# Chunk spacing, accumulator banks and the order of small vector work in a hybrid S5 and retention layer

## The chip, the core and the metric

The kernel runs on one NeuronCore of a Trainium2 chip. The metric is the device time of one execution in microseconds (us); the kernel before has a median of 1449.79 us over three runs (1449.29 to 1450.3). The engines are called by the names of the profile: PE (matmul), DVE (vector), ACT (scalar), POOL (GpSimd) and SP (here used for issuing DMAs).

## The reference

One layer of a decoder is computed for 256 prompt positions and for 8 sequences of 8 decode positions, 320 token columns in all, in float32. The shape of the work, cut to what matters here:

```python
h = rms_norm(x, norm_mix)
u, q, k, v, g = split(h @ w_in)                      # 2048 x 5120
bu = einsum('nlgh,gph->lngp', ug, ((lam_bar-1)/lam)[..., None] * b)
xs = associative_scan(a = lam_bar, bu)               # complex diagonal state, 64 groups x 64
y = gelu(Re(c @ xs) + d*u);  s5_out = y * sigmoid(y @ w_glu + b_glu)
o = chunked retention with decay (8 heads, rotary q and k), group norm, silu(g) gate
x = x + concat([s5_out, ret_out]) @ w_out            # 2048 x 2048
x = x + (silu(h2 @ w_gate) * (h2 @ w_up)) @ w_ffn_out  # 2048 x 2*5632, then 5632 x 2048
y = rms_norm(x);  the last S5 and retention states are returned too
```

Weights are fetched as float32 and split into two parts (`hi`, `lo`); each product is the sum of three matmuls (hi by hi, hi by lo, lo by hi).

## The kernel before

**Dense products.** `gemm` (L137) goes through 128-row tiles of the contraction, called k-steps here. A k-step is three matmuls of 128x128 by 320 columns (L143 to L145). `wload` (L122) issues a 512 KB load of 8 k-steps of weights on SP, a cast to `hi` on ACT (L131) and the subtraction that gives `lo` on DVE (L133). There are three buffers each of raw, `hi` and `lo`, so weights run at most three tiles ahead of PE. An output tile accumulates in a PSUM bank of the pool `ps_acc`, tag "acc", with two buffers.

**The stages in order.** First the input projection: a head (L917 to L943) that computes four output tiles together (two S5 inputs, q and k of head 0) as x and the weights arrive; then v of head 0, and the loop L985 over eight heads with q, k, v, for the first four heads also the gate g, for the first six also one S5 input tile u; then the last four gates. Second the first half of the output projection, `ps_o`, on the retention rows: `gemm_late` (L151) takes its first two output tiles together and goes through heads 0 to 3 of both before heads 4 to 7 of both. Third the GLU product, the second half of the output projection, and the FFN.

**What is woven between.** During the input projection, PE also does the small matmuls of the retention heads (`head_k` L711, `head_v` L736) and of eight S5 chunks (`s5_chunk` L575). PE's and POOL's orders are written out by hand: a planner keeps a clock, `clk.now`, that each matmul advances by a fixed cost (0.4 for a k-step); a generator that yields a number of units is resumed at the first k-step boundary after its due time (`run_due`, L91). Chunk c is due to start at `T0 + PER*c` (L978). From its start it yields `b1` = 14.2 (then `pt`, transposes of the input matrix `bl`), `b2` = 6.6 (then `pb`, the product with the inputs `kst`, and `pk_`, the local kernel `toe`), `scan` = 17.8 (then `py`, the output product) and `y` = 10 (then the elementwise end). When the input projection is over, a loop (L1010) runs the planner on, without dense work between, until chunk 7 is done; only then the output projection is written to PE's stream. The DVE, ACT and SP orders are not fixed by hand: the framework orders them when the program is built, by program order less an offset where one is given (`tc.high_priority`), and by `tc.issue_after`, which puts a block behind a named instruction on its engine. An engine executes its queue in that order.

**PSUM.** Eight banks: two for `ps_acc`; three for `ps_m`, tag "misc", which hold the small results of heads and chunks (`pst`, `pss`, `pst2`, `psr`, `pn`, `pt`, `pk_`, the norm sums, and the v product of head 0); one for `ps_v` (`po`); two for `ps_b` (`pb` and `py` in turn). In the head, `py0` is a "misc" bank, `pb0` the two of `ps_b`, and `pk0` an "acc" bank beside that of the warming matmuls.

**S5 parameters and tables.** `s5_params` (L382), `s5_params2` (L422) and `s5_params3` (L444) make the powers of the transition from small tiles, on DVE; `s5_params2` stands behind the scaling of the rotary tables (L969), `s5_params3` behind the scores of head 0 (L732). `first_states` (L468) is six POOL multiplications and additions that the planner starts at `T0 + 1`. `s5_table` (L517) makes a chunk's rotation table with six DVE operations, right behind its matrices (L612).

**The first loads.** ACT issues the parameter vector `vec` (L918) and the second k-step's weights, SP the first k-step's x, the first weights, and all further loads.

Of the kernel before, what the change touches and what calls it, by code (L numbers as in the profile page):

```python
# [12 lines left out]
F32 = mybir.dt.float32  # L13
# [5 lines left out]
PSUM = bass.MemoryType.PSUM  # L19

P = 128
# [3 lines left out]
N = NP + NB * NS  # L25
# [19 lines left out]
def hybrid_kernel(ctx, tc, xT, w_in, w_in4, w_out, w_glu, w_fi, w_fo, vecs, s5p, bc, x0,  # L45
# [3 lines left out]
    pe, act, dve, pool, sp = nc.tensor, nc.scalar, nc.vector, nc.gpsimd, nc.sync  # L49

    cst = ctx.enter_context(tc.tile_pool(name="cst", bufs=1))
    wp = ctx.enter_context(tc.tile_pool(name="wp", bufs=1))
    ps_acc = ctx.enter_context(tc.tile_pool(name="ps_acc", bufs=2, space=PSUM))

    def f(t):
        return t.bitcast(F32)
# [8 lines left out]
    vec = cst.tile([P, vecs.shape[1]], F32, name="vec")  # L65
# [18 lines left out]
    clk = Clk()  # L84
# [6 lines left out]
    def run_due(flush=False):  # L91
        while clk.heap and (flush or clk.heap[0][0] <= clk.now):
            t, _, gen = heapq.heappop(clk.heap)
            clk.now = max(clk.now, t)
            try:
                d = next(gen)
            except StopIteration:
                continue
            spawn(gen, d)
# [11 lines left out]

    def keep_warm(n):

        pt = ps_acc.tile([P, 512], F32, name="warm_ps", tag="acc", bufs=2)
        for _ in range(n):
            pe.matmul(pt, onesr, onesr.unsqueeze(1).to_broadcast([P, 4, P]), start=True, stop=True)

# [19 lines left out]
    def gemm(name, src, nk, xhi, xlo, ps=None, ws=None):  # L137
        ws = ws or wload(src, nk)
        if ps is None:
            pt = ps_acc.tile([P, 512], F32, name=name, tag="acc", bufs=2)  # L140
            ps = pt[:, :N]
        for k, (hi, lo) in enumerate(ws):
            pe.matmul(ps, hi, xhi[:, k], start=k == 0, stop=False)  # L143
            pe.matmul(ps, hi, xlo[:, k], start=False, stop=False)  # L144
            pe.matmul(ps, lo, xhi[:, k], start=False, stop=k == nk - 1)  # L145
            clk.now += 0.4
            if k < nk - 1:
                run_due()
        return ps

    def gemm_late(name, src, n0, ks, nk, xhi, xlo):  # L151

        ws = [wload(src(n0 + i), nk) for i in range(2)]
        pss = []
        for k0, k1 in ((0, ks), (ks, nk)):
            for i in range(2):
                if not k0:
                    pss.append(ps_acc.tile([P, 512], F32, name=name, tag="acc", bufs=2)[:, :N])
                for k in range(k0, k1):
                    hi, lo = ws[i][k]  # L160
                    pe.matmul(pss[i], hi, xhi[:, k], start=k == 0, stop=False)
                    pe.matmul(pss[i], hi, xlo[:, k], start=False, stop=False)
                    pe.matmul(pss[i], lo, xhi[:, k], start=False, stop=k == nk - 1)
                    clk.now += 0.4
                    if k < nk - 1:
                        run_due()
        return pss


    def ts(out, a, s1, o1, s2=None, o2=None):  # L170
        if o2 is None:
            dve.tensor_scalar(out, a, s1, None, o1)
        else:
            dve.tensor_scalar(out, a, s1, s2, o1, o2)
        return out

    def tt(out, a, b, op):
        dve.tensor_tensor(out, a, b, op)  # L178
        return out
# [51 lines left out]
    retpool = ctx.enter_context(ExitStack())  # L231
# [1 line left out]
    xgstack = ExitStack()  # L233
    xg = xgstack.enter_context(tc.tile_pool(name="xg", bufs=1))
    mp = retpool.enter_context(tc.tile_pool(name="mp", bufs=1, side="right"))
    ps_m = retpool.enter_context(tc.tile_pool(name="ps_m", bufs=3, space=PSUM))
    ps_v = retpool.enter_context(tc.tile_pool(name="ps_v", bufs=1, space=PSUM))
    up = retpool.enter_context(tc.tile_pool(name="up", bufs=1, side="right"))
    s5 = s5stack.enter_context(tc.tile_pool(name="s5", bufs=1, side="right"))
# [1 line left out]
    ps_b = s5stack.enter_context(tc.tile_pool(name="ps_b", bufs=1, space=PSUM))  # L241

    def misc(name):
        return ps_m.tile([P, 512], F32, name=name, tag="misc", bufs=3)

    xhi = xg.tile([P, KT, N], F32R, name="xhi")
    xlo = xg.tile([P, KT, N], F32R, name="xlo")
# [86 lines left out]
    def T(shape):  # L334
        n = int(np.prod(shape[1:]))
        a = scr[0][:, scr[1]:scr[1] + n]
        scr[1] += n
        if len(shape) == 3:
            a = a.rearrange("p (a b) -> p a b", b=shape[2])
        return a  # L340
# [81 lines left out]
    def s5_params2(used):  # L422
        newscr(1)
        scr[1] = used
        tt(lp[:, 0, 0], rr, ec[:, 0], MUL)
        tt(lp[:, 1, 0], rr, es[:, 0], MUL)
        den = tt(T(sh), prm[:, 0], prm[:, 0], MUL)
        d2 = tt(T(sh), prm[:, 1], prm[:, 1], MUL)
        tt(den, den, d2, ADD)
        rden = T(sh)  # L430
        dve.reciprocal(rden, den)
        nr = ts(T(sh), lp[:, 0, 0], -1.0, ADD)
        t1 = tt(T(sh), nr, prm[:, 0], MUL)
        t2 = tt(T(sh), lp[:, 1, 0], prm[:, 1], MUL)
        tt(t1, t1, t2, ADD)
        tt(ff[:, 0], t1, rden, MUL)
        t3 = tt(T(sh), lp[:, 1, 0], prm[:, 0], MUL)
        t4 = tt(T(sh), nr, prm[:, 1], MUL)
        tt(t3, t3, t4, SUB)
        tt(ff[:, 1], t3, rden, MUL)  # L440
        r2 = tt(T(sh), rr, rr, MUL)
        tt(r4, r2, r2, MUL)

    def s5_params3():  # L444
        def cmul(o, a, b, shape, tt=tt):

            u1, u2 = T(shape), T(shape)
            tt(u1, a[0], b[0], MUL)
            tt(u2, a[1], b[1], MUL)
            tt(o[0], u1, u2, SUB)  # L450
            tt(u1, a[0], b[1], MUL)
            tt(u2, a[1], b[0], MUL)
            tt(o[1], u1, u2, ADD)

        def ri(t, i):
            return (t[:, 0, i], t[:, 1, i])

        def rep_(t, n):
            return tuple(t[:, q].unsqueeze(1).to_broadcast([P, n, NPAIR]) for q in range(2))

        cmul(ri(lp, 1), ri(lp, 0), ri(lp, 0), sh)
        cmul(ri(lp, slice(2, 4)), rep_(lp[:, :, 1], 2), ri(lp, slice(0, 2)), [P, 2, NPAIR])
        cmul(ri(gp, slice(0, 3)), rep_(ff, 3), ri(lp, slice(0, 3)), [P, 3, NPAIR])

        def b8(a):
            return a.unsqueeze(2).to_broadcast(shx)

        def first_states():  # L468

            yield max(0.0, T0 + 1.0 - clk.now)  # L470
            newscr(0)
            cmul((lx0[:, 0], lx0[:, 1]), (x0t[:, 0], x0t[:, 1]), (b8(lp[:, 0, 3]), b8(lp[:, 1, 3])), shx,
                 pool.tensor_tensor)

        spawn(first_states())
# [99 lines left out]
    def s5_chunk(c):  # L575
# [14 lines left out]
        raw = raws[c]  # L590
# [7 lines left out]
        for w_, pc in ((0, gpc), (1, lpc)):  # L598
# [10 lines left out]
                continue  # L609
            tt(cl[:, 0], m1[:, 0:4], m2[:, 4:8], SUB)  # L610
            tt(cl[:, 1], m1[:, 4:8], m2[:, 0:4], SUB)
        tbl = s5_table(c)  # L612
        yield DL["b1"] + (4.0 if c == 0 else 0.0)
        bst = s5.tile([P, 4, P], F32, name="bst", tag="bst", bufs=1)
        pt = misc("pt")
        for i in range(4):
# [77 lines left out]
    rot_t = {}  # L694
# [197 lines left out]
    def do_g(h):  # L892
        ps = proj(11 + 4 * h)
        sg = mp.tile([P, N], F32, name="sg", tag="sg", bufs=2)
        with tc.high_priority(offset=EVAC):
# [5 lines left out]

    DL = dict(b1=14.2, b2=6.6, scan=17.8, y=10.0, k=8.5, v=6.1,
              o=2.2, u=6.0, c=10.0, n2=2.4, n2b=2.6, nm=0.8)
    T0, PER = 53.6, 33.4


    clk.now = 8.0
# [1 line left out]
    warm = cst.tile([P, 1], F32, name="warm")  # L909
    act.activation(warm, ones[:, 0:1], AF.Silu)  # L910

    py0 = misc("py0")
    pb0 = ps_b.tile([P, 2, 512], F32, name="pb0", tag="pb", bufs=1)
    keep_warm(8)
    pk0 = ps_acc.tile([P, 512], F32, name="ps_p", tag="acc", bufs=2)
    accs = [py0[:, :N], pb0[:, 0, :N], pb0[:, 1, :N], pk0[:, :N]]
    with tc.high_priority(offset=100000), tc.manual_schedule(engines={mybir.EngineType.SP}):  # L917
        act.dma_start(vec, vecs)  # L918
    k0, los = 0, []
    for k1 in (1, *range(2, KT + 1, 2)):  # L920
        with tc.high_priority(offset=100000), tc.manual_schedule(engines={mybir.EngineType.SP}):
            if k0 % 2 == 0:
                raw, hi, lo = (wp.tile([P, 8, P], d, name=n, tag=n, bufs=3).rearrange("p (k o) m -> p k o m", o=4)
                               for n, d in (("raw", F32), ("hi", F32R), ("lo", F32R)))
            q = slice(k0 % 2, (k1 - 1) % 2 + 1)
            sp.dma_start(xrs[k0 // 4][:, k0 % 4:(k1 - 1) % 4 + 1], xT[:, k0:k1])
            (act if k0 == 1 else sp).dma_start(raw[:, q], w_in4[:, k0:k1])
            if k1 == 4:
                sp.dma_start(prm, s5p)
            split_x(k0, k1)  # L930
            act.copy(hi[:, q], raw[:, q])
            los.append(dve.tensor_tensor(lo[:, q], raw[:, q], f(hi[:, q]), SUB))
        if k1 == 4:
            exps = s5_exps()
        if k1 % 2 == 0:
            with tc.high_priority(offset=50000):
                accq = square_x(k1 - 2, k1)
        for k in range(k0, k1):
            for w_, x_ in ((hi, xhi), (hi, xlo), (lo, xhi)):
                for i, ps in enumerate(accs):  # L940
                    pe.matmul(ps, w_[:, k % 2, i], x_[:, k], start=k == 0 and w_ is hi and x_ is xhi,
                              stop=k == KT - 1 and w_ is lo)
            clk.now += 1.6  # L943
        k0 = k1
# [384 lines left out]
```

## Time and profile before

| what | value |
|---|---|
| median of three runs | 1449.79 us |
| the profiled execution | 1448.5 us |
| its span, first to last instruction | 1446.7 us |
| PE busy | 1427.1 us (99%) |
| DVE busy | 849.1 us (59%) |
| ACT busy | 600.7 us (42%) |
| mean granted TensorE clock | 0.995 |

The span is what the trace shows; the execution's own time has 1.8 us around it. Busy time of PE counts overlapping, modelled matmul spans, so that idle time is read from the waits and from the starts of successive matmuls. A timeline row gives the start, the length of the stretch of that group, the engine, the line, the output and inputs, the shape and, in brackets, how long the engine sat idle before and what ended it.

### The profile page before, as it was taken

What the parts mean: (1) busy time and instruction counts of PE and PEld (TensorE: products, weight loads), DVE (VectorE), ACT (ScalarE), POOL (GpSimd) and SP (SyncE); (2) the same over time, 40 slices, a digit from 0 to 9 for tenths busy, and PEclk for the clock granted to TensorE, in tenths of its full rate; (3) what the DMA queues carried; (4) which work ended last, traced back from release to release, by engine and by line L of the source; (5) the groups of instructions that cost most, each with busy time, mean ns of one, the idle gap of its engine ahead of it and who ended that gap; (6) DMA issues with size and microseconds to landing.
All of it is one profiled execution on the core that took longest, in us unless ns stands there. A gap on an engine that the chain in (4) does not pass through costs nothing.

```text
span 1446.7 us, 25879 instructions
## 1 busy us (share of the span) xinstructions
PE 1427.1 (99%) x10434; PEld 1413.5 (98%) x10434; DVE 849.1 (59%) x1378; ACT 600.7 (42%) x945; POOL 75.1 (5%) x161
## 2 busy tenths in 40 slices
PE   9999999998999999999999999999999999999997
PEld 9999999998999999999999999999999999999996
DVE  8978877786566746565444444444444444444454
ACT  7645555554355533333333333333333333333452
POOL 7610000010000000000000000000000000000001
PEclk9999999999999999999999999999999999999998
DMA  8555555555544576664445445444445444444542
GB/s 290 167 162 167 156 172 157 170 155 178 160 154 151 186 222 189 219 202 162 146 152 155 121 145 182 150 146 152 125 149 169 157 154 146 140 138 143 156 145 111
DMA packets 92774, 235.09 MB, mean 163 GB/s; under 512 B 26480, under 2 KB 40432, under 8 KB 92656
## 3 DMA queue, kind: packets, MB, share of 16 engines
q1 hardware_dynamic: 91600, 231.06, 50.3%
q10 hardware_dynamic: 1056, 2.40, 0.5%
q8 instruction: 82, 1.34, 0.4%
q14 instruction: 36, 0.29, 0.1%
HBM read 220.66 MB, written 10.26 MB: 160 GB/s over the span
## 4 chain that ended last, share of the span: by engine, by line
PE 70%; DVE 0%; issue 0%; ACT 0%; DVEq 0%
PE ps_fg L143 7%; PE ps_fo L145 7%; PE ps_fu L145 7%; PE ps_fg L145 7%; PE ps_fo L144 7%; PE ps_fu L144 7%; PE ps_fu L143 7%; PE ps_fg L144 7%; PE ps_fo L143 7%; PE ps_o L144 1%; PE ps_o L143 1%; PE ps_o L145 1%; PE ps_g L144 1%; PE ps_g L145 1%; PE ps_g L143 1%; DVE x L178 0%
## 5 line engine op out<-in xcount | busy, mean ns | idle before, releaser
L133 DVE TENSOR_TENSOR lo<-raw,hi 128x1024 fp32r<-128x1024 f32 (+1 forms) x416 | 467.0, 1123 | 384.0 <-ACT hi L131 383.0
L131 ACT CAST hi<-raw 128x1024 fp32r<-128x1024 f32 (+1 forms) x416 | 401.8, 967 | 683.1 <-PE ps_fo L144 189.3
L143 PE MATMUL ps_fg<-hhi,hi 128*128 128x320 f32 x704 | 217.6, 309 | 0.0
L144 PE MATMUL ps_fo<-alo,hi 128*128 128x320 f32 x704 | 217.5, 309 | 0.0
L145 PE MATMUL ps_fo<-ahi,lo 128*128 128x320 f32 x704 | 217.5, 309 | 0.0
L143 PE MATMUL ps_fo<-ahi,hi 128*128 128x320 f32 x704 | 217.5, 309 | 0.0
L145 PE MATMUL ps_fg<-hhi,lo 128*128 128x320 f32 x704 | 217.4, 309 | 0.0
L144 PE MATMUL ps_fu<-hlo,hi 128*128 128x320 f32 x704 | 217.4, 309 | 0.0
L143 PE MATMUL ps_fu<-hhi,hi 128*128 128x320 f32 x704 | 217.4, 309 | 0.0
L145 PE MATMUL ps_fu<-hhi,lo 128*128 128x320 f32 x704 | 217.4, 309 | 0.0
L144 PE MATMUL ps_fg<-hlo,hi 128*128 128x320 f32 x704 | 217.4, 309 | 0.0
L143 PE MATMUL ps_p<-xhi,hi 128*128 128x320 f32 x560 | 177.8, 318 | 1.3 <-DVE q__1070 L178 1.3
L145 PE MATMUL ps_p<-xhi,lo 128*128 128x320 f32 x560 | 173.1, 309 | 0.0
L144 PE MATMUL ps_p<-xlo,hi 128*128 128x320 f32 x560 | 172.9, 309 | 0.0
L144 PEld LDWEIGHTS ps_fg<-hlo,hi 128*128 128x128 f32 x704 | 132.4, 188 | 0.4
L143 PEld LDWEIGHTS ps_fg<-hhi,hi 128*128 128x128 f32 x704 | 132.3, 188 | 0.3
L143 PEld LDWEIGHTS ps_fu<-hhi,hi 128*128 128x128 f32 x704 | 132.4, 188 | 0.0
L144 PEld LDWEIGHTS ps_fu<-hlo,hi 128*128 128x128 f32 x704 | 132.4, 188 | 0.0
L145 PEld LDWEIGHTS ps_fu<-hhi,lo 128*128 128x128 f32 x704 | 132.4, 188 | 0.0
L145 PEld LDWEIGHTS ps_fg<-hhi,lo 128*128 128x128 f32 x704 | 132.3, 188 | 0.0
L143 PEld LDWEIGHTS ps_fo<-ahi,hi 128*128 128x128 f32 x704 | 132.2, 188 | 0.0
L144 PEld LDWEIGHTS ps_fo<-alo,hi 128*128 128x128 f32 x704 | 132.2, 188 | 0.0
(420 smaller groups left out, 1909.9 us busy)
## 6 DMA issues: line engine op xcount, KB each, us to landing
raw<-w_fi SPq DMA_DIRECT2D x176, 512.0 KB, 3.7
raw<-w_in SPq DMA_DIRECT2D x79, 512.0 KB, 3.9
raw<-w_fo SPq DMA_DIRECT2D x64, 512.0 KB, 3.5
raw<-w_out SPq DMA_DIRECT2D x32, 512.0 KB, 3.7
raw<-w_fo SPq DMA_DIRECT2D x64, 192.0 KB, 2.4
rt<-r SPq DMA_DIRECT2D x8, 512.0 KB, 4.9
raw<-w_glu SPq DMA_DIRECT2D x8, 512.0 KB, 3.5
raw<-r SPq DMA_DIRECT2D x8, 512.0 KB, 4.3
```

Source lines behind the costliest of these rows:

```text
L131: cast = act.copy(hi[:, :m], raw[:, :m])
L133: dve.tensor_tensor(lo[:, :m], raw[:, :m], f(hi[:, :m]), SUB)
L143: pe.matmul(ps, hi, xhi[:, k], start=k == 0, stop=False)
L144: pe.matmul(ps, hi, xlo[:, k], start=False, stop=False)
L145: pe.matmul(ps, lo, xhi[:, k], start=False, stop=k == nk - 1)
```

## The change

- `PER`, the spacing of the S5 chunks on the planner's clock, goes from 33.4 to 32.0.
- `ps_acc` has three buffers, `ps_m` two. `py0` of the head moves from "misc" to "acc".
- The second half of `s5_params2` (eleven small DVE operations that make `ff` and `r4`) moves to the beginning of `s5_params3`, which stands behind the scores of head 0.
- For chunk 0, `s5_table` is called after the chunk's first yield.
- `first_states` is due at `T0 + 12` on the planner's clock in place of `T0 + 1`.
- ACT issues the first k-step's weights; `vec` and the second k-step's weights go to SP, `vec` behind the first x.

```diff
-    ps_acc = ctx.enter_context(tc.tile_pool(name="ps_acc", bufs=2, space=PSUM))
+    ps_acc = ctx.enter_context(tc.tile_pool(name="ps_acc", bufs=3, space=PSUM))
...
-    ps_m = retpool.enter_context(tc.tile_pool(name="ps_m", bufs=3, space=PSUM))
+    ps_m = retpool.enter_context(tc.tile_pool(name="ps_m", bufs=2, space=PSUM))
...
         dve.reciprocal(rden, den)
+        rot_t["rden"] = rden
+
+    def s5_params3():
+        rden = rot_t["rden"]
         nr = ts(T(sh), lp[:, 0, 0], -1.0, ADD)
...
         tt(r4, r2, r2, MUL)
 
-    def s5_params3():
         def cmul(o, a, b, shape, tt=tt):
...
-            yield max(0.0, T0 + 1.0 - clk.now)
+            yield max(0.0, T0 + 12.0 - clk.now)
...
-        tbl = s5_table(c)
+        if c:
+            tbl = s5_table(c)
         yield DL["b1"] + (4.0 if c == 0 else 0.0)
+        if not c:
+            tbl = s5_table(c)
...
-    T0, PER = 53.6, 33.4
+    T0, PER = 53.6, 32.0
...
-    py0 = misc("py0")
+    py0 = ps_acc.tile([P, 512], F32, name="py0", tag="acc", bufs=3)
...
-    with tc.high_priority(offset=100000), tc.manual_schedule(engines={mybir.EngineType.SP}):
-        act.dma_start(vec, vecs)
...
             sp.dma_start(xrs[k0 // 4][:, k0 % 4:(k1 - 1) % 4 + 1], xT[:, k0:k1])
-            (act if k0 == 1 else sp).dma_start(raw[:, q], w_in4[:, k0:k1])
+            (sp if k0 else act).dma_start(raw[:, q], w_in4[:, k0:k1])
+            if not k0:
+                sp.dma_start(vec, vecs)
```

The other lines of the diff give the accumulators' tiles `bufs=3` and the "misc" tiles `bufs=2`.

More of the change, by code (lines that the diff above doesn't have):

```diff
@@ L112, in keep_warm @@
     def keep_warm(n):
-        pt = ps_acc.tile([P, 512], F32, name="warm_ps", tag="acc", bufs=2)
+        pt = ps_acc.tile([P, 512], F32, name="warm_ps", tag="acc", bufs=3)
         for _ in range(n):
@@ L139, in gemm @@
         if ps is None:
-            pt = ps_acc.tile([P, 512], F32, name=name, tag="acc", bufs=2)
+            pt = ps_acc.tile([P, 512], F32, name=name, tag="acc", bufs=3)
             ps = pt[:, :N]
@@ L157, in gemm_late @@
                 if not k0:
-                    pss.append(ps_acc.tile([P, 512], F32, name=name, tag="acc", bufs=2)[:, :N])
+                    pss.append(ps_acc.tile([P, 512], F32, name=name, tag="acc", bufs=3)[:, :N])
                 for k in range(k0, k1):
@@ L243, in misc @@
     def misc(name):
-        return ps_m.tile([P, 512], F32, name=name, tag="misc", bufs=3)
+        return ps_m.tile([P, 512], F32, name=name, tag="misc", bufs=2)
     xhi = xg.tile([P, KT, N], F32R, name="xhi")
@@ L910, in hybrid_kernel @@
     act.activation(warm, ones[:, 0:1], AF.Silu)
-    py0 = misc("py0")
+    py0 = ps_acc.tile([P, 512], F32, name="py0", tag="acc", bufs=3)
     pb0 = ps_b.tile([P, 2, 512], F32, name="pb0", tag="pb", bufs=1)
     keep_warm(8)
-    pk0 = ps_acc.tile([P, 512], F32, name="ps_p", tag="acc", bufs=2)
+    pk0 = ps_acc.tile([P, 512], F32, name="ps_p", tag="acc", bufs=3)
     accs = [py0[:, :N], pb0[:, 0, :N], pb0[:, 1, :N], pk0[:, :N]]
-    with tc.high_priority(offset=100000), tc.manual_schedule(engines={mybir.EngineType.SP}):
-        act.dma_start(vec, vecs)
     k0, los = 0, []
```

## The prediction

> **What bounds the kernel now.** The page first, then what PE waited for:
>
> ```profile
> span 1446.7 us, 25879 instructions
> PE   9999999998999999999999999999999999999997
> PE py L102 <- ACT endp L564: 2.9, 1, 2.9
> PE ps_p L143 <- DVE q__1070 L178: 1.3, 1, 1.3
> ...
> PE py L102 <- DMA toe<-toe: 1.1, 1, 1.1
> PE po L102 <- DVE sm L178: 1.0, 1, 1.0
> ```
>
> Each digit is a tenth of PE's busy share in one of 40 slices. PE works without a break but for a handful of waits, each of which came once (columns: who waited for whom; us in total, times, longest). No faster engine helps elsewhere; the question is which of these waits go and what ends last in their place. Two of those shown, and a third of 0.3, belong to `py` of the last S5 chunk. The timeline of PE there, with one ordinary crossing from dense work through `py` of chunk 6 and back ahead of it (the first two rows), and two windows for the clock:
>
> ```profile
> 328.26 0.31 PE L145 MATMUL ps_p<-xhi,lo 128*128 128x320 f32 x1
> 329.49 0.41 PE L143 MATMUL ps_p<-xhi,hi 128*128 128x320 f32 x1
> 344.54 0.78 PE L102 MATMUL pb<-kst,bst 64*64 64x80 f32 x32
> 346.24 0.31 PE L145 MATMUL ps_p<-xhi,lo 128*128 128x320 f32 x1
> 346.68 0.31 PE L145 MATMUL ps_p<-xhi,lo 128*128 128x320 f32 x1
> 349.85 0.53 PE L102 MATMUL py<-kst,toe 64*64 64x80 f32 x4 [2.87 <-ACT endp L564]
> 352.60 1.41 PE L102 MATMUL py<-xp,cl 64*64 64x80 f32 x32 [0.35 <-DVE xp L178]
> 353.94 0.63 PE L161 MATMUL ps_o<-r4a,hi 128*128 128x320 f32 x1
> 355.70 0.42 PE L161 MATMUL ps_o<-r4a,hi 128*128 128x320 f32 x1
> 70.00:80.00 10.00, 8.73 (x60) 8.47 (x59) 9.90 (x18) 2.94 (x4) 3.19 (x4) 1.00 0.43 128
> 354.00:356.00 2.00, 2.00 (x10) 2.00 (x9) 2.00 (x7) 0.47 (x1) 0.00 (x0) 0.52 0.87 314
> ```
>
> `pb` of chunk 7 stands shortly before the end of the dense stream: the input projection's last matmul starts at 346.68 and the retention product starts at 353.94. A window's columns are busy time by engine, then granted clock, DMA share and GB/s: after the break the clock stood at 0.52.
>
> **The chunk spacing.** Chunk 7 is due at 53.6 + 7 × 33.4 = 287.4 units of the planner; with 32.0 at 277.6, 9.8 units earlier. A k-step is 0.4 units, so its `pb` moves 24 k-steps up PE's stream. The rows at 346.24 and 346.68 end successive k-steps: 0.44 us each. In the old stream two k-steps follow `pb`; in the new one 26, or 11.4 us of dense work. What has to fit under it is the scan: from `pb` (344.54) to the first product with `xp` (352.60) it took 8.1 us, with little else on DVE. Among dense work chunk 6 took longer:
>
> ```profile
> 306.72 0.78 PE L102 MATMUL pb<-kst,bst 64*64 64x80 f32 x32
> 316.07 0.75 DVE L178 TENSOR_TENSOR xp<-v,v 128x252 f32<-128x252 f32 x2
> ```
>
> that is 316.82 − 306.72 = 10.1 us, without the higher priority that chunk 7 has. Either fits into 11.4. So the break closes: 346.68 to 353.94 is 7.26 us, an ordinary crossing 329.49 − 328.26 = 1.23, a gain of 6.0. From 353.94 to 355.70 PE started six more matmuls in 1.76 us at the low clock; at 0.147 each (0.44 over three) they take 0.9. **Tail: −6.0 − 0.9 = −6.9 us** (0 to −6.9).
>
> [...]
>
> Chunks 2 to 6 move up by 1.4 units per chunk; their inputs u are written a head or more ahead of their start in either order, and no wait of PE's lies between 76 and 346 us. I take 0 for them; the bound is under the rivals.
>
> **What is late next at the tail.** The operands of heads 4 to 7 (`r4b`) are made after the dense stream has ended:
>
> ```profile
> 347.95 0.82 ACT L1045 CAST r4b<-retp 128x320 fp32r<-128x320 f32 x2
> 351.64 0.48 DVE L178 TENSOR_TENSOR sg<-ps_p,rbc 128x320 f32<-128x320 f32 x1
> 353.10 1.70 DVE L178 TENSOR_TENSOR r4b<-retp,r4b 128x320 fp32r<-128x320 f32 x4
> ```
>
> They had 11 us under the break. New: after the end T, `py` takes 1.1, heads 0 to 3 of two output tiles eight k-steps (3.5), so head 4 is wanted at T + 4.6 and head 7 three k-steps later, T + 5.9. DVE owes by then the gate (0.48), a product (0.48, as the read of q at 76.03 below), four subtractions (1.70) and one weight subtraction (1.2): 3.9 us, in an order that I can't see. It fits, narrowly. **+0.4** (0 to +2).
>
> **Scores ahead of parameters, tables later, third accumulator.** The two early waits, and what DVE did before them:
>
> ```profile
> 51.52 0.42 DVE L172 TENSOR_SCALAR scrt<-lp 128x32 f32<-128x32 f32 x1
> 57.32 0.61 DVE L178 TENSOR_TENSOR sm<-pss,mk 128x256 f32<-128x256 f32 x2
> 69.44 1.76 DVE L133 TENSOR_TENSOR lo<-raw,hi 128x1024 fp32r<-128x1024 f32 x1
> 71.91 0.31 PE L145 MATMUL ps_p<-xhi,lo 128*128 128x320 f32 x1
> 72.85 1.79 DVE L178 TENSOR_TENSOR e<-e 128x256 f32<-128x256 f32 x4
> 74.89 1.21 DVE L133 TENSOR_TENSOR lo<-raw,hi 128x1024 fp32r<-128x1024 f32 x1
> 76.03 0.48 DVE L178 TENSOR_TENSOR q__1070<-ps_p,csr 128x320 f32<-128x320 f32 x1
> 76.56 0.42 PE L143 MATMUL ps_p<-xhi,hi 128*128 128x320 f32 x1 [1.26 <-DVE q__1070 L178]
> ```
>
> The scores `sm` are done at 57.93, and PE had waited 1.0 for them, from 56.9. The eleven operations that go behind them begin at 51.52; that first one took 0.42 with the wait for its input, and at only 0.2 each, an estimate at half of that, they are 2.2 us. The scores come at about 55.7 and the wait goes. But DVE is full here (9.90 of 10 us in the window from 70) and has the same sum of work before the weights at 69.44: those are ready at 71.20, PE wants them at 71.91. PE can arrive at most 0.7 earlier: **−0.7**, not −1.0. The table (`e`, 1.79, and `tb`) leaves DVE's queue ahead of 74.89 for one after the chunk's first yield; the weights and the read of q then come some 2 us earlier, and with a third accumulator PE needn't wait for q at all. The 1.26 goes: **−1.3**. The table is wanted only at `pb` of chunk 0, ahead of which DVE has gaps. Bounds of the two together: 0 (other work takes the slots) to −2.4.
>
> The third accumulator hides nothing else: the list of waits has one for `ps_p`. The two "misc" banks cost a wait where a third tile comes before the first is read out. Head 0 has such a place:
>
> ```profile
> 53.49 0.36 ACT L720 ACTIVATE kv<-pst,kdc 64x128 f32<-64x128 f32 x1
> 53.66 0.44 PE L107 MATMUL pst<-ident,v__747 128*128 128x128 f32 x2
> 290.01 0.21 DVE L730 TENSOR_TENSOR smp<-pss,mk 64x64 f32<-64x64 f32 x1
> 290.59 0.49 PE L107 MATMUL pst<-ident,v__3972 128*128 128x128 f32 x3
> ```
>
> `pst` is read out at 53.85, the third tile starts at 53.66: +0.2, hidden in the 0.3 that the weights at 69.44 take back anyway. In head 6 even the later-read scores are free at 290.22, before 290.59. I take 0 (0 to +13, a rival below).
>
> `first_states` moves on the planner's clock, but POOL has nothing else between its old place (behind head 0's norm) and its new one, and POOL's queue waits for data alone: 0. [...]
>
> **The first loads.** ACT's rows and PE's third k-step:
>
> ```profile
> 1.17 0.45 ACTq L927 DMA_DIRECT2D raw<-w_in  x1
> 4.97 0.62 ACT L931 CAST hi<-raw 128x512 fp32r<-128x512 f32 x1 [1.82 <-DMA raw<-w_in]
> 8.23 1.05 ACT L931 CAST hi<-raw 128x1024 fp32r<-128x1024 f32 x1
> 9.33 0.41 PE L941 MATMUL py<-xhi,hi 128*128 128x320 f32 x1
> ```
>
> The first weights are issued one slot (0.45) earlier, so PE may start 0.45 earlier; but its third k-step starts as the cast of 8.23 ends (9.28), and those weights now stand one slot later in SP's queue, behind `vec` and the second k-step. What is won is waited off there: **+0.1** (−0.5 to +0.5, a slot either way).
>
> **The sum.** −6.9 + 0.4 − 0.7 − 1.3 + 0.1 = −8.4 us. The profiled execution took 1448.5 (span 1446.7 and 1.8 around it), so 1440.1 by it; the median shown, 1449.8, lies 1.3 above, and I forecast against it: **1441.4 us**, a span near 1438.3.
>
> **Rivals.** *Half a tail* (0.13): the scan of chunk 7 or `r4b` waits in a DVE queue for weight casts or elementwise ends of chunk 6. For it: DVE's order is not written by hand, and `sg` at 351.64 stood 4.6 us behind its product (346.68 + 0.31). Against: 10.1 against 11.4. A remnant of 3.0 and the clock's 0.9: 1441.4 + 3.9 = **1445.3**.
>
> *The spacing does nothing* (0.08): DVE, ACT and SP follow program order and not PE's; should chunk 7's matrices or inputs come as late as before, `py` waits as before and only the early terms are left: 1449.8 − 1.9 = **1447.9**, which a measurement can't tell from no change (within 0.2%, 2.9 us).
>
> *The lost bank* (0.09), on the slower side: eight heads and eight chunks each put a tile behind the scores or the normed output, which DVE reads. With two banks PE, in order, waits for DVE wherever it is late. At 0.8 us in each of 16 places, 12.8 us: 1441.4 + 12.8 = **1454.2**. It decides from 11.3 us on, 0.7 a place. For it: PE had gone on from head 0's scores at 53.66, and DVE read them at 57.32. Against: head 6 above, where the slowest of the later heads still is in time.
>
> **Chances.** Forecast 0.70, half a tail 0.13, spacing idle 0.08, lost bank 0.09. Faster by over 0.2% are the first two: 0.83; same 0.08; slower 0.09. All bounds on the good side (tail −6.9, early −2.4, head −0.5) give −9.8 and 1440.0, by the profiled execution's base 1438.7; the low end, with half a us for the spread of the runs, is 1438.2. The high end takes in half a tail: 1446.4. The forecast's own range is 1438.2 to 1444.
>
> **What would show it.** Right: no `py` wait near the end of the input projection, the clock at 1.00 through it, first `ps_o` about 9 us earlier, no `po` or `ps_p` wait before 80 us, unchanged spacing of matmuls between 80 and 330. Wrong: `ps_o` waiting for `r4b`; PE rows that wait with ACT or DVE ahead of `pst`, `pt`, `pn` or `pk_`; a third k-step later than 9.3.

## The result and the profile after

The changed kernel takes 1441.53 us (median of 4, 1440.78 to 1442.48), the kernel before, timed beside it, 1449.54 (1448.77 to 1450.3): a ratio of 0.9944, interval 0.9928 to 0.9959. The forecast was 1441.4. The profiled execution took 1440.78 us. First its page, and what PE waited for:

```profile
span 1438.9 us, 25723 instructions
PE   9999999999999999999999999999999999999997
...
PE py L947 <- ACT hi L937: 0.6, 1, 0.6
PE ps_p L145 <- DVE lo L133: 0.4, 2, 0.2
PE ps_g L144 <- DVE ylo L182: 0.3, 1, 0.3
PE pst L107 <- ACT kv L726: 0.2, 1, 0.2
```

The slice of 8, in which the input projection ended, is a 9 now. The waits of `po` for the scores, of `ps_p` for q and of `py` for `endp` and `toe` are gone; a wait for the weight subtraction (`lo`) and one for `kv` have come. "Crossing" below is the time from the last matmul of the input projection to the first of the output product. PE's timeline at `pb` and `py` of chunk 7, the window that held the low clock, and the last `xp` on DVE:

```profile
332.61 0.78 PE L102 MATMUL pb<-kst,bst 64*64 64x80 f32 x32
345.63 0.31 PE L145 MATMUL ps_p<-xhi,lo 128*128 128x320 f32 x1
345.87 0.52 PE L102 MATMUL py<-kst,toe 64*64 64x80 f32 x15
346.91 0.42 PE L161 MATMUL ps_o<-r4a,hi 128*128 128x320 f32 x1
...
354.00:356.00 2.00, 2.00 (x16) 2.00 (x15) 1.86 (x3) 1.05 (x1) 0.00 (x0) 1.00 1.01 413
...
339.31 0.75 DVE L178 TENSOR_TENSOR xp<-v,v 128x252 f32<-128x252 f32 x2
```

From the projection's last matmul to the first output product it is 1.28 us, where it was 7.26. `xp` is written 7.5 us after `pb` (340.06 − 332.61), 5.8 before `py` begins. The early part:

```profile
9.77 0.41 PE L947 MATMUL py<-xhi,hi 128*128 128x320 f32 x1 [0.63 <-ACT hi L937]
...
71.60 0.42 PE L145 MATMUL ps_p<-xhi,lo 128*128 128x320 f32 x1 [0.22 <-DVE lo L133]
74.92 0.31 PE L143 MATMUL ps_p<-xhi,hi 128*128 128x320 f32 x1
75.40 0.48 DVE L178 TENSOR_TENSOR q__1052<-ps_p,csr 128x320 f32<-128x320 f32 x1
```

The third k-step starts 0.44 later than before (9.33); the tile that had waited 1.26 for q starts at 74.92, ahead of the reading of q at 75.40, as the third accumulator allows.

To compare traces, PE's stream is cut at four matmuls that every kernel has: the start of the third k-step of the head; a matmul of the input projection behind all early waits (at 81.21 us before, 79.98 after); the projection's last matmul; the 21st matmul of the output product (357.87 before), at which the clock was back in every trace. The table gives the five stretches in us, the last up to the last matmul of the last product, each a difference of two starts in the trace. "bc" is explained under the early part.

| kernel | head | early | bc | dense | tail | rest |
|---|---|---|---|---|---|---|
| before | 9.33 | 71.88 | 27.84 | 265.47 | 11.19 | 1072.98 |
| after | 9.77 | 70.21 | 28.09 | 265.65 | 4.33 | 1072.98 |
| spacing alone | 11.39 | 71.89 | 27.91 | 265.65 | 4.44 | 1072.98 |
| all but spacing | 9.90 | 70.59 | 28.78 | 265.47 | 11.92 | 1072.99 |
| spacing 33.0 | 9.76 | 70.06 | 27.80 | 265.57 | 10.48 | 1072.99 |
| spacing 31.0 | 9.77 | 71.92 | 30.12 | 268.16 | 4.75 | 1072.98 |
| 31.0, old first loads | 10.68 | 70.49 | 28.50 | 268.37 | 4.27 | 1072.99 |
| old first loads | 10.26 | 70.53 | 28.58 | 265.65 | 4.66 | 1072.98 |
| two loads on ACT | 10.15 | 71.83 | 30.50 | 265.65 | 5.25 | 1072.98 |
| old banks | 9.24 | 74.08 | 30.97 | 265.65 | 4.90 | 1072.98 |
| old banks, again | 10.16 | 71.36 | 28.96 | 265.65 | 4.57 | 1072.99 |
| old table | 9.69 | 70.69 | 28.76 | 265.65 | 4.27 | 1072.99 |
| old parameters | 9.93 | 71.14 | 27.92 | 265.65 | 4.27 | 1072.99 |
| toe copies first | 10.06 | 70.84 | 29.06 | 265.65 | 4.27 | 1074.02 |

Between the pair: +0.44 − 1.67 + 0.18 − 6.86 + 0 = −7.91, of the spans' −7.8. "Dense" repeats to 0.01 among the kernels with a spacing of 33.4, and among those with 32.0, and "rest" in all but the last row; "head" and "early" do not, and there one pair of traces proves little.

### The profile page after: what moved, and what is told of

Read it like the earlier page. It is cut to its first block, busy times and chain, and to the rows that moved or that the text cites. A ratio compares the mean times of both kernels' runs of the same rounds, so it can differ in the third digit from the quotient of the medians.

```text
span 1438.9 us, 25723 instructions
## 1 busy us (share of the span) xinstructions
PE 1425.4 (99%) x10434; PEld 1411.7 (98%) x10434; DVE 847.6 (59%) x1378; ACT 600.2 (42%) x945; POOL 75.1 (5%) x161
## 3 DMA queue, kind: packets, MB, share of 16 engines
HBM read 220.66 MB, written 10.26 MB: 160 GB/s over the span
## 4 chain that ended last, share of the span: by engine, by line
PE 71%; DVE 1%; ACT 0%; issue 0%; DVEq 0%
PE ps_fo L144 7%; PE ps_fu L144 7%; PE ps_fu L145 7%; PE ps_fo L143 7%; PE ps_fu L143 7%; PE ps_fo L145 7%; PE ps_fg L143 7%; PE ps_fg L144 7%; PE ps_fg L145 7%; PE ps_o L144 1%; PE ps_o L143 1%; PE ps_o L145 1%; PE ps_g L144 1%; PE ps_g L145 1%; PE ps_g L143 1%; DVE x L178 0%
```

## The experiments

### The tail: spacing alone, all but spacing, 33.0 and 31.0

Kernel before, spacing alone:

```diff
-    T0, PER = 53.6, 33.4
+    T0, PER = 53.6, 32.0
```

> The kernel before with the spacing alone changed from 33.4 to 32.0. Theory (the break at the last chunk closes by the spacing and by nothing else): the first output product (ps_o) starts 6.0 us earlier than in the kernel before, near 347.9, the clock stays at 1.00 there, and the end comes 6.9 us earlier: 1442.6 us. The waits of 1.0 (po) and 1.26 (ps_p for q) before 80 us stay, and the last row of the input projection stays near 346.7. Rival (the early edits are needed too, because DVE comes late into the chunks' chain without them): a wait of py for endp or xp of 1 to 4 us is left at chunk 7, and the time is 1445 to 1448.

Changed kernel, spacing back:

```diff
-    T0, PER = 53.6, 32.0
+    T0, PER = 53.6, 33.4
```

> The changed kernel with the spacing back at 33.4. Theory: the break of 7.3 us ahead of the first output product is there again, with the low clock behind it; only the early terms are left, about -1.1 us at the last row of the input projection (345.6): 1448.5 us. Rival (the third accumulator or the freed DVE slots shorten the last chunk's chain as well): the break is under 5 us and the time is 1446 or less.

Measured: 1442.97 us (ratio to before 0.995, 0.9933 to 0.9966) for the spacing alone, and 1448.83 (0.9993, 0.9984 to 1.0003) for all the rest. PE's timeline with the spacing alone, then without it:

```profile
348.92 0.31 PE L145 MATMUL ps_p<-xhi,lo 128*128 128x320 f32 x1
...
350.33 0.41 PE L161 MATMUL ps_o<-r4a,hi 128*128 128x320 f32 x1
```

```profile
345.96 0.31 PE L145 MATMUL ps_p<-xhi,lo 128*128 128x320 f32 x1
349.16 0.35 PE L102 MATMUL py<-kst,toe 64*64 64x80 f32 x4 [2.89 <-ACT endp L567]
351.01 0.80 PE L102 MATMUL py<-kst,toe 64*64 64x80 f32 x12 [1.50 <-DMA toe<-toe]
```

The tail follows the spacing and nothing else: 4.44 with it, 11.92 without. The rivals, that the early edits are needed for it or shorten the chain themselves, fall. The absolute starts that were expected are missed by 2 us with the spacing alone because that execution's head was 2 us later, on unchanged code (the cause is under the head). By the times, all the rest without the spacing is not told from no change; what it gains is read from the traces below.

A value between, 33.0 in the place of 32.0:

> The changed kernel with the spacing at 33.0. Chunk 7 is due 2.8 units earlier than at 33.4, that is 7 k-steps of 0.44: nine k-steps follow its pb instead of 2. Theory (each k-step behind pb covers 0.44 us of the scan, up to the 7.26 us break): the break between the last row of the input projection and the first output product is 7.26 - 3.1 = 4.2 us, of which 1.2 are the ordinary crossing, and PE's clock stays at 1.00 as the wait ahead of py is under 1 us: 3.0 us lost against the changed kernel, 1444.5 us. Rival (the thin work by itself lowers the clock, or the scan's order in DVE's queue gives all or nothing): 0.9 more (1445.4), or a break of over 6 or under 2 us.

Measured 1446.5 us (0.9976, 0.9967 to 0.9986): neither. PE's timeline, and windows of a microsecond, in which the last column but two is the granted clock:

```profile
345.39 0.31 PE L145 MATMUL ps_p<-xhi,lo 128*128 128x320 f32 x1
346.20 0.36 PE L102 MATMUL py<-kst,toe 64*64 64x80 f32 x4 [0.50 <-PE ps_p L145]
348.00 0.49 PE L102 MATMUL py<-kst,toe 64*64 64x80 f32 x12 [1.44 <-DMA toe<-toe]
349.27 1.41 PE L102 MATMUL py<-xp,cl 64*64 64x80 f32 x32 [0.78 <-DVE xp L178]
350.61 0.63 PE L161 MATMUL ps_o<-r4a,hi 128*128 128x320 f32 x1
...
348.00:349.00 1.00, 0.49 (x12) 0.33 (x12) 1.00 (x2) 0.24 (x1) 0.00 (x0) 0.87 0.68 233
349.00:350.00 1.00, 0.73 (x20) 0.76 (x24) 1.00 (x4) 0.11 (x1) 0.00 (x0) 0.50 0.96 277
355.00:356.00 1.00, 1.00 (x6) 1.00 (x6) 0.97 (x4) 0.43 (x1) 0.00 (x0) 0.72 1.04 430
```

The break is 5.22 us (350.61 − 345.39), not 4.2: the scan, with dense work and its casts on DVE beside it, took 1.2 longer than under the bare break (`pb` at 340.2, `xp` complete at 349.5). And the clock fell, at a cost of 2.2 us, not 0.9: from the first to the 21st output product it took 5.26 us against 3.05. So two thirds of the break remain, and with the clock most of the loss: 10.48 of tail, against 11.92 with all but the spacing and 11.19 before. The clock did not fall every time: its mean over the execution is 0.995 or 0.996, as before, in eight of the ten executions, and 0.998, as in the changed kernel, in two (1446.46 and 1444.41 us, the latter near the theory).

The other side, 31.0:

> The changed kernel with the spacing at 31.0. Chunk 7 is due another 7 units, 17 k-steps or 7.5 us, earlier. Theory (at 32.0 the scan fits already; what is left there is the last two toe copies, which stand behind two weight loads in SP's queue and have some 1 us to spare): the crossing from the last row of the input projection to the first output product is 1.2 to 1.3 us, as in the changed kernel, without any wait of py for toe; the time is that of the changed kernel less at most 0.5: 1441.0 to 1441.5. Rival (chunks that stand closer collide on DVE with the heads' work): waits of py for endp, ends or xp or of ps_p for lo between 80 and 340 us, 1442.5 or more.

Measured 1445.28 us (0.9971, 0.9959 to 0.9982): the time of the rival, but not its wait, and the theory's crossing failed too (1.71, not 1.2 to 1.3). The dense stretch is 2.5 longer. The one large wait there is of `py` at chunk 6, for its `toe` copies and not for the scan; below it SP's queue ahead of it:

```profile
315.86 0.42 PE L102 MATMUL py<-kst,toe 64*64 64x80 f32 x10 [1.55 <-DMA toe<-toe]
...
304.48 1.88 SPq L648 DMA_DIRECT2D toe<-toe  x3
311.02 0.36 SPq L130 DMA_DIRECT2D raw<-w_in  x1
311.48 1.87 SPq L648 DMA_DIRECT2D toe<-toe  x3
```

Three of the chunk's `toe` copies stand behind a weight load that can't be issued before its buffer is free; SP stands from 306.4 to 311.0, 4.6 us in which it waited for a `lo` on DVE. `pss` waits twice for `bst` besides (0.3 in all). Some 0.7 of the 2.5 goes with no single wait and stays open, and so does the rest of the 3.8 by which the medians differ. 32.0 thus lies between two losses, a scan that doesn't fit and copies that come late.

### What is late next: the toe copies first

In the changed kernel too two of chunk 7's copies stand behind two weight loads:

```profile
334.77 3.21 SPq L648 DMA_DIRECT2D toe<-toe  x4
339.45 2.12 SPq L130 DMA_DIRECT2D raw<-w_out  x2
341.63 1.25 SPq L648 DMA_DIRECT2D toe<-toe  x2
```

With 32.0, `py` waited for them in two traces (0.6 with two loads on ACT, 0.3 with the old banks); the third that the expectation counts has only a crossing of 1.61 to show for it. The changed kernel with:

```diff
+        with tc.high_priority(offset=2 * EVAC if c == 7 else 0):
             for u in range(2):
                 for t in range(CH - 1):
...
                     sp.dma_start(toe[64 * u + d:64 * u + 64, :, t], toe[64 * u:64 * u + 64 - d, :, CH - 1])
```

> The changed kernel (spacing 32.0) with chunk 7's toe copies given the priority of its scan, so that all six stand ahead of the two weight loads in SP's queue. Theory (the toe copies, not r4b, are late next at the tail; three of seven traces with 32.0 waited 0.3 to 0.6 for them): the copies land 4 us or more before py needs them, the crossing is 1.23 to 1.3 us, the time 1441.2 to 1441.5, that is -0.3 in the mean of many runs and nothing against the best. Rival (the weight loads that are pushed back come late in turn): ps_o waits for hi or lo after 346 us, 1442.5 or more.

Measured 1442.4 us (0.995, 0.9933 to 0.9967). The crossing is 1.23 (347.79 after 346.56), as expected, but the time isn't better. DVE's timeline there, and PE's first waiting row:

```profile
347.90 0.79 DVE L182 SCALAR_TENSOR_TENSOR y<-u,vec,yc 128x320 f32<-128x320 f32 x1 [1.07 <-DMA yc<-back]
348.61 0.48 DVE L178 TENSOR_TENSOR sg<-ps_p,rbc 128x320 f32<-128x320 f32 x1
...
350.74 0.49 DVE L178 TENSOR_TENSOR r4b<-retp,r4b 128x320 fp32r<-128x320 f32 x1
...
352.49 0.42 PE L162 MATMUL ps_o<-r4b,hi 128*128 128x320 f32 x1 [0.77 <-DVE r4b L178]
```

Three loads of chunk 6's `yc` went back behind the copies in SP's queue, the last one behind two weight loads as well; `y` waited for them on DVE, and behind `y` in its queue stand `sg` and `r4b`. PE then waited for `r4b`: 0.77 by the row, 1.0 in all ("rest" 1074.02 against 1072.98). The rival's time is nearly there (1442.5 or more was expected), with `r4b` in the place of `hi` or `lo`. This is the prediction's step for `r4b`, in another kernel than the one it was made for.

### The head: the order of the first loads

Changed kernel, old order:

```diff
+        act.dma_start(vec, vecs)
...
-            (sp if k0 else act).dma_start(raw[:, q], w_in4[:, k0:k1])
-            if not k0:
-                sp.dma_start(vec, vecs)
+            (act if k0 == 1 else sp).dma_start(raw[:, q], w_in4[:, k0:k1])
```

> The changed kernel with the order of the first loads of the kernel before (ACT issues vec and the second weights, SP the first). Theory (the late weight subtractions on DVE set PE's time near 71 and 79 us, as in the prediction's step for po): PE starts 0.66 us later, its third k-step comes back to 9.33 (0.44 earlier than in the changed kernel), but PE then waits 0.4 us longer at the subtractions, and the last row of the input projection stays within 0.15 of 345.63: 1441.5 us. Rival (the 0.44 goes straight through to the end): the last row is at 345.2 and the time 1441.1.

Second weights on ACT too:

```diff
-            (sp if k0 else act).dma_start(raw[:, q], w_in4[:, k0:k1])
+            (sp if k0 > 1 else act).dma_start(raw[:, q], w_in4[:, k0:k1])
```

> The changed kernel with the second weights issued by ACT too, behind the first, so that the third weights stand fifth in SP's queue instead of sixth. Theory: PE's first k-step starts as in the changed kernel, near 5.0, the third at 9.3 and not 9.77; by the theory of the late subtractions the last row of the input projection nevertheless stays within 0.15 of 345.63 (1441.5 us). Rival (what is won at the head goes straight through): 345.2 and 1441.1 us.

Measured 1442.06 us (0.9944, 0.9929 to 0.9959) and 1441.54 us (0.9944, 0.993 to 0.9959): no difference from the changed kernel that these times tell. Both expectations for the third k-step failed: it came at 10.26 and 10.15, not 9.33. ACT's rows for the old order show why; in the trace of before the same `xhi` (at 5.52) had waited for nothing:

```profile
4.96 0.62 ACT L937 CAST hi<-raw 128x512 fp32r<-128x512 f32 x1 [1.81 <-DMA raw<-w_in]
6.44 0.56 ACT L271 ACTIVATE xhi<-u,vec 128x320 fp32r<-128x320 f32 x1 [0.86 <-DMA u<-xT]
```

The landing of the first x, not the issue slot, set the head in this trace. The theory tested there falls as well: it had the late weight subtractions fix PE's time at 71 and 79 us, so that a change at the head would be waited off. But "early" is 70.53 with the old loads against 70.21: the later head of this trace is not made up for by 81 us.

31.0 with the old order:

> The same (31.0) with the first loads in the order of the kernel before. Theory (the first loads' new order wins some 0.6 us in the mean, which the one profile of before hides: the third k-step started at 9.33, 11.39 and 10.26 in three traces of the old order and at 9.24 to 9.93 in six of the new one): the third k-step at 9.8 or later, and the median 0.3 to 1.0 above that of the run with 31.0 and the new order. Rival (the order costs 0.4, as the first pair of traces says): the third k-step at 9.4 or earlier, the median 0.4 lower.

The third k-step came at 10.68, as expected (there a later x landed late), but the median, 1445.21 us (0.9968, 0.9957 to 0.998), is that of the new order (1445.28), not above it. By the traces the old order gives 9.33, 10.26, 10.68 and 11.39, in the mean 10.42; the new one, nine times, 9.24 to 10.16, in the mean 9.81. The 0.6 between the means was the theory, but the 11.39, of the spacing alone, is not the work of the loads. That trace's cast for the third k-step, and PE:

```profile
8.82 1.03 ACT L931 CAST hi<-raw 128x1024 fp32r<-128x1024 f32 x1
...
9.11 0.47 PE L941 MATMUL py<-xhi,hi 128*128 128x320 f32 x1
9.38 0.73 PE L941 MATMUL pb<-xhi,hi 128*128 128x320 f32 x2
...
11.39 0.31 PE L941 MATMUL py<-xhi,hi 128*128 128x320 f32 x1
```

The weights were cast by 9.85, but PE was late. Its matmuls started 0.27 us apart up to 10.18, where they start 0.15 apart later on and in the trace of before: PE ran at the low clock, as from 354.37 to 355.44 in the trace of before, where they start 0.27 apart and a window's granted clock is 0.50. The first rise of the clock stands in the trace's clock record at 10.26, and at 4.36 in that of before (ahead of the first record a window's column says 1.00, so that there only the spacing of the matmuls tells). The other three of the old order have a mean of 10.09, 0.3 above the new one, and spread over 1.35. So it is not shown which order is better, and no pair of medians tells them apart.

### The early part: banks, table, parameters

Changed kernel with two accumulators and three misc banks (`py0` of the head in a misc bank again); the table ahead of the first yield; the eleven operations in the function ahead of the scores:

```diff
-    ps_acc = ctx.enter_context(tc.tile_pool(name="ps_acc", bufs=3, space=PSUM))
+    ps_acc = ctx.enter_context(tc.tile_pool(name="ps_acc", bufs=2, space=PSUM))
-    ps_m = retpool.enter_context(tc.tile_pool(name="ps_m", bufs=2, space=PSUM))
+    ps_m = retpool.enter_context(tc.tile_pool(name="ps_m", bufs=3, space=PSUM))
...
```

> The changed kernel with two accumulators and three misc banks as before (py0 in a misc bank again). All milestones are read against the third k-step's start in the same trace, because the head differed by up to 2 us between runs of one and the same code in the first four experiments. Theory (the third accumulator, not the later table, takes the 1.26 us wait away): in the changed kernel q is read out at 75.88 while PE starts the next tile at 74.92, so with two accumulators a wait of about 1.0 for q comes back; the wait of 0.2 of the third misc tile behind kv goes; the last row of the input projection stands 0.7 to 0.9 later against the third k-step than in the changed kernel (335.9 there). Rival (the later table did it): no wait for q, and the distance is 335.7 to 335.9.

```diff
-        if c:
-            tbl = s5_table(c)
+        tbl = s5_table(c)
         yield DL["b1"] + (4.0 if c == 0 else 0.0)
-        if not c:
-            tbl = s5_table(c)
```

> The changed kernel with the table of chunk 0 in its old place, ahead of the chunk's first yield. Theory (the third accumulator does it): no wait for q, at most 0.3 more at the weight subtractions, the distance from the third k-step to the last row of the input projection 335.9 to 336.2. Rival (the table's place is needed): the weights' subtractions or q come 1 us or more later and PE waits 0.7 us or more in 70 to 82.

```diff
         dve.reciprocal(rden, den)
-        rot_t["rden"] = rden
-
-    def s5_params3():
-        rden = rot_t["rden"]
         nr = ts(T(sh), lp[:, 0, 0], -1.0, ADD)
...
         tt(r4, r2, r2, MUL)
+
+    def s5_params3():
```

> The changed kernel with the parameters' eleven operations ahead of the scores again. Theory (the prediction's step): the wait of po for sm, 1.0 to 1.7, comes back at 57 to 60, and the waits for the weight subtractions near 71 and 79 (0.2 to 0.6 in the three kernels with the change's early edits and no other wait) go, so that the last row of the input projection stands 0.6 to 1.1 later against the third k-step than 335.9. Rival (the two cancel wholly, DVE being the bound until 80): within 0.2 of 335.9.

One execution each: 1444.62, 1441.09 and 1441.64 us. The old banks gave a surprise, a wait of 2.4 for k. ACT's rows of that trace, then the same of the changed kernel:

```profile
40.21 1.06 ACT L596 ACTIVATE cz<-raw_bc 64x64 f32<-64x64 f32 x4 [3.63 <-DMA raw_bc<-bc]
41.29 1.05 ACT L131 CAST hi<-raw 128x1024 fp32r<-128x1024 f32 x1
```

```profile
37.86 1.06 ACT L596 ACTIVATE cz<-raw_bc 64x64 f32<-64x64 f32 x4 [1.58 <-DMA raw_bc<-bc]
```

The second `raw_bc` landed late, and ACT, in order, held the weights' cast behind it, DVE the subtraction, and q and k behind that. "bc" in the table is the start of this `cz` against the third k-step. "Early" follows it: over the nine kernels with scores ahead and three accumulators (the old table among them) it goes from 70.06 at 27.80 to 70.84 at 29.06 and about 71.9 at 30.1 and 30.5. So kernels have to be compared at equal "bc". That its lateness is the cause (in three traces POOL's `scrt` ended that wait, in the others the transfer) is argued from the queues; no kernel moved `cz`. In this trace of the old banks the wait for k also lowered the clock, which cost another 1.4 (the last section has the rows), so that its 74.08 says little of the banks, and the 0.7 to 0.9 that was expected could not be read from it. The old banks once more:

> The kernel of the earlier run with the old banks, once more, as there a transfer of raw_bc landed 2.4 us later than in the changed kernel and held the casts behind it on ACT. Theory (that lateness was of the one execution; the third accumulator takes the wait for q away, and in the earlier run it would have covered the late k as well): no wait of ps_p for k, a wait of 0.6 to 1.0 for q, none of pst for kv, the last row of the input projection 336.4 to 336.9 after the third k-step. Rival (two accumulators bring the wait for k by themselves once the scores stand ahead): a wait for k of over 1 us again.

Measured 1442.54 us; the waits of that trace:

```profile
PE ps_p L143 <- DVE q__1052 L178: 1.2, 1, 1.2
...
PE ps_p L143 <- DVE k__729 L178: 0.4, 1, 0.4
```

Between theory and rival: q's wait is back in full, none for `kv`, but a small one for k is left without the late landing, the last row of the projection (337.01 after the third k-step) is above the 336.9 expected, and "early" is 71.36, where three accumulators have about 70.8 at that "bc". By this trace the third accumulator is worth 0.6; the first hints at more when DVE is late. The old table: 70.69 at 28.76, against 70.59 at 28.78 with the new place, and no wait for q, as the theory said (the last row of the projection, 336.33 after the third k-step, is just above the 336.2 expected): by this pair of traces the table's place is worth 0.1. The old parameters: 71.14 at 27.92, against 70.06 and 70.21; `po` waits again, as expected, which is 1.0. With the 0.6 and the 0.1 that is the 1.7 of the whole; each of the three rests on one trace:

```profile
58.53 0.91 PE L102 MATMUL po<-vT,sm 128*128 128x128 f32 x6 [0.95 <-DVE sm L178]
```

## Why the prediction was right, step by step

**Chunk spacing: right.** −6.86 of tail between the pair, predicted −6.9; `pb` moved the 24 k-steps that were worked out, and two experiments give the whole tail to the spacing. In the dense stretch it costs 0.18, not 0: 265.47 in both traces with 33.4, 265.65 in all nine with 32.0.

**The low clock behind the break: right for the trace of before, its price no constant.** 0.9 there, 1.6 in the trace of all but spacing (11.92 − 7.26 = 4.66 from the first to the 21st output product, against 3.05), 2.2 with 33.0, and 1.4 at the wait for k. "Half a tail" was priced as 3.0 + 0.9; a break partly closed can lose more, as the 33.0 shows. That half a break costs the whole 0.9 was the author's estimate; with 33.0 a break of 5.22 cost the 2.2. A wait of 2.44 between dense products (first trace of the old banks) lowered the clock as well.

**What is late next: right in kind, wrong in size and name.** +0.4 for `r4b` was 0 in the changed kernel; 1.0 when `y` came late. The nearer limit, the `toe` copies behind weight loads in SP's queue, was not in the prediction.

**Early waits: −2.0 predicted, −1.67 between the pair**, and at equal "bc" −1.7 to −1.8 (70.06 and 70.21 against 71.88 and 71.89). The wait for `sm` and the wait for q went, as said, and the subtraction at 69.89 limited PE, as said. Not in the sum was what came back: a second wait for `lo` at 75.54 (0.16), and a slower step behind a wait (71.60 to 71.85, 0.25, where the steps around it take 0.15). The two terms were both mis-sized, and in their sum the errors cancel in part, which is luck: −0.7 for the scores, where the old parameters cost 1.0; −1.3 for table and accumulator together, where single traces give 0.1 and 0.6. So the accumulator did most of that, and less than the whole wait.

**The misc bank: right.** The wait at head 0 is there in every trace with two misc banks, 0.2 or 0.3. The rival of the lost bank falls: the dense stretch, with all later heads and chunks, is 265.65 with two misc banks and with three (spacing alone, old banks).

**`first_states`: right as far as seen.** POOL's instructions stand in the same order in both kernels. It was not run by itself.

**First loads: +0.1 predicted, inside its ±0.5 for the pair (+0.44), open for the kernel.** In the pair the mechanism is there in full: the third k-step's cast starts at 8.68 where it started at 8.23, a slot later. In other traces the landing of x, or the clock, set the head, and they don't show which order is better.

**The base.** The forecast stood 1.3 above the sum because the profiled execution lay that far under its median. Why it did is not shown; its head, the earliest of the four with the old order, is a candidate. That forecast and measured median agree to 0.1 is luck in part: the change gained 8.0, not 8.4, and the median of before, timed beside it, was 0.25 lower than the one used. The "span near 1438.3" goes with the 1440.1 and not with the forecast.

**The signs.** The `py` waits went, the clock stayed at 1.00, and the unchanged code between 80 and 330 us kept its pace but for the 0.18. Others failed. The first output product came 7.0 earlier (353.94 to 346.91) and not about 9, where the prediction's own terms give 7.9; and `ps_p` still waits twice before 80 us. Two of the signs of being wrong came, a third k-step later than 9.3 and a wait of `pst` for ACT, both small.

## What to carry to other kernels

A planner's spacing has two ends: too wide and the last chain doesn't fit under the dense work (here a break of 7.26 us at 33.4), too close and the copies of the chunk queue behind loads that wait for buffers (SP stood for 4.6 us at 31.0); a point in between is found by counting what follows the last chunk's start against its chain. A break that is only partly closed may gain little (here 1.4 of the 7.6 us of tail at 33.0, by the traces), because the clock can fall all the same, as it did there, and then more of the dense work runs under it (2.2 us lost, 0.9 in the trace of before). Before a step of half a microsecond is read off a pair of traces, cut the stream at fixed matmuls and see, in traces of other kernels with the same code there, how much that stretch varies by itself.

## What the runs showed of the hardware that was not expected

The low clock lasted equally long in three traces. Windows of the kernel before, then of all but spacing:

```profile
349.00:350.00 1.00, 0.15 (x2) 0.18 (x4) 1.00 (x2) 0.64 (x3) 0.00 (x0) 0.55 0.04 4
355.00:356.00 1.00, 1.00 (x6) 1.00 (x5) 1.00 (x5) 0.47 (x1) 0.00 (x0) 0.53 0.85 305
```

```profile
349.00:350.00 1.00, 0.35 (x4) 0.22 (x4) 1.00 (x2) 0.00 (x0) 0.00 (x0) 0.99 0.11 11
356.00:357.00 1.00, 1.00 (x6) 1.00 (x6) 0.97 (x4) 0.47 (x1) 0.00 (x0) 0.59 1.02 420
```

The whole windows between the two have 0.50 in both traces, and with 33.0. With the clock at 0.50 or 1.00 in each part of such a window, the fall and the rise lie at 349.10 and 355.94 before, 349.98 and 356.82 in the second, and 348.74 and 355.56 with 33.0: 6.84, 6.84 and 6.82 us, though different work ran under it. In the first trace of the old banks it was half of that:

```profile
52.09 0.41 PE L143 MATMUL ps_p<-xhi,hi 128*128 128x320 f32 x1 [2.44 <-DVE k__729 L178]
...
52.00:53.00 1.00, 0.91 (x5) 0.91 (x6) 1.00 (x4) 0.00 (x0) 0.95 (x2) 0.78 0.37 49
...
55.00:56.00 1.00, 1.00 (x6) 1.00 (x5) 0.89 (x3) 0.00 (x0) 1.00 (x2) 0.51 0.01 2
```

The fall lies at 52.56, the rise at 55.98, 3.42 us later. In between twelve dense matmuls took 3.20 us, where 0.147 each makes 1.76: the 1.4 named above. What sets these lengths no run shows.

The fall did not stand at one place against the wait: in the trace of before dense work ended at 346.99 and the fall came 2.1 us later, within the wait of 2.87; at the wait for k it came 0.47 behind the wait's end at 52.09. The wait of 1.55 us at 315.86 with the spacing at 31.0 did not lower the clock:

```profile
314.00:316.00 2.00, 0.45 (x12) 0.32 (x15) 2.00 (x5) 0.93 (x2) 0.00 (x0) 1.00 0.53 85
```

So a wait of 1.55 us left the clock up there, and waits of 2.44 (for k), 2.87 (before) and 2.89 (all but spacing) went with a fall; with 33.0 it was waits of 0.50, 1.44 and 0.78 with thin work between. What decides no run shows.

The other surprise is how much transfers of unchanged code vary in landing. The second `raw_bc` came 27.8 to 31.0 us after the third k-step, and by the traces more than half of that reached PE. The third k-step itself came at 9.24 to 10.68, the trace with the late clock aside. The dense stretch, at one spacing of 33.4 or 32.0, and the last stretch repeat to a hundredth.
